# Moving mLSTM's half of the branch merge next to its gates, with the attention's halves made late

## The chip, the cores and the metric

The kernel runs on one core of a Trainium2 chip. The metric is the device time of one execution, in microseconds. Before the change the median of three runs is 1825.51 us (1820.42 to 1829.21).

## The reference

One block of a diffusion transformer over 512 tokens of width 1024 (with 256 context tokens): a token mixer with two branches, mLSTM (4 heads of 128) and window attention (8 query heads of 64, blocks of 128 tokens), a merge of the two behind sigmoid gates, a projection, and then PEER, a mixture of 16,384 tiny experts. The six modulation vectors (shift, scale and gate of both halves) come from `silu(c) @ w_ada`.

```python
mod = jax.nn.silu(cond) @ w + b                      # w: 1024 x 6144
pl = _split_in(h_lat @ w_in)
m_lat, m_ctx = _mlstm_branch(pl[:5], pc[:5], b_mgates, mlstm_norm_g, with_ctx_out)
a_lat, a_ctx = _attn_branch(pl[5:8], pc[5:8], q_g, k_g, sink, cos, sin, with_ctx_out)

def merge(m, a, gates):
    g_m, g_a = jnp.split(gates, 2, axis=-1)
    return (jax.nn.sigmoid(g_m) * (m @ w_bm) + jax.nn.sigmoid(g_a) * (a @ w_ba)) @ w_out

x = x + g1 * y_lat
x = x + g2 * _peer(_modulate(x, norm_ffn_g[layer], sh2, sc2), ...)
```

## The kernel before

**Arithmetic.** Every large product is float32 made of three passes: each operand is split into a high half (a copy rounded by ScalarE, `split`, L51) and a low half (the difference, L52, on VectorE or GpSimd), and `mm3` (L182 to L185) issues high x high, low x high and high x low. A tile product of 128 x 128 by 128 x 512 is therefore three matmuls.

**Stages.** (1) Norm, modulation and the projections of q, k, v and the attention's inputs. (2) The mLSTM heads (L503 to L537): for each head and direction a masked decay matrix `dm` (L510 to L513), two products per chunk and a running state; then the normaliser `den` and the norm over `num` (L541 to L559). (3) Attention (L586 to L643): the keys and queries are transposed and split; for each of four blocks `n` there are scores for 8 heads (L607, L608), a softmax (L615 to L626), transposes of the probabilities (L632) that are copied to `pTs` by VectorE and ScalarE in turn (L635, L637), and the product with the values (L640) into `po`; `split(ahi, alo, po)` ends a block. (4) Gates: `gate_proj` (L651) loads 0.5 MB of `w_gate`, splits it on ScalarE and GpSimd, and makes 24 matmuls into one PSUM bank: 4 output gates of mLSTM into `sigo`, then 16 branch gates (8 column tiles `n`, two branches `br` each), which are stored to DRAM (`sgd`, L681). After `sigo`, `num` is transposed (L670), scaled into `mt` (L672) and split to `mhi`, `mlo`. (5) Merge (L690 to L713): for each `n` the two gates are loaded again (`sgm`, L693), 0.5 MB of `w_br` is loaded and split, both branches' products are made (12 matmuls each), multiplied by the gates on VectorE (L710, L711), added on GpSimd (L712) and split to `zhi`, `zlo`. (6) Projection by `w_out` (L738 to L750): 24 matmuls for each of 8 column tiles, the residual (L749), squares, and a transposed copy. (7) The PEER stage follows and has its own written order.

**What sets the order.** Up to the PEER stage a scheduler orders each engine's instructions from the program order (earlier code has precedence) and from when it expects operands; at run time each engine and the DMA queue of SyncE (SP) work their list strictly in order. So gate products, written after the attention, fill TensorE's list between the attention's steps. Three background jobs are spread through these stages. `adas` (L138) loads one 0.5 MB row block of the modulation weights (`wada`, two buffers) and reduces it against `silp` on VectorE (`dot`, L134): 12 in the head loop (L540) and 20 in the attention loop (L643). `ahead(n)` (L352) prepares n tiles of the expert weights for PEER: load 0.5 MB (`sraw`, L358), high half on ScalarE (L360), low half on VectorE (L361), and, at the next call, store of the low half (`lows`, L355): 4 with the output gates, 16 with the branch gates, 8 in the merge, 8 in the projection. Weight tiles share one pool: `wraw` for loads, three buffers each of `whi` and `wlo`.

Of the kernel before, what the change touches and what calls it, by code (L numbers as in the profile page):

```python
# [38 lines left out]
def body(ctx, tc, A, out):  # L39
# [61 lines left out]
    silp = ga([128, 2, D], F32, "sil")  # L101

# [30 lines left out]
    def dot(w, i, col, keep=False):  # L133
        junk = wb([128, D], mybir.dt.bfloat16, "junk") if keep else w  # L134
        V.tensor_tensor_reduce(out=junk, in0=w, in1=silp[:, i], scale=1.0, scalar=0.0,  # L135
                               op0=ALU.mult, op1=ALU.add, accum_out=col)
# [428 lines left out]
    amask = ga([128, 640], F32, "amask")  # L565
# [25 lines left out]
    ahi, alo = ga([128, NB, 4, 128], F32R, "ahi"), ga([128, NB, 4, 128], F32R, "alo")  # L591
    for n in range(4):
# [49 lines left out]
        split(ahi[:, n], alo[:, n], po)  # L642
# [22 lines left out]
    g_m = load_const("g_mlstm", [128, 4])  # L665
    mhi, mlo = ga([128, NH, T], F32R, "mhi"), ga([128, NH, T], F32R, "mlo")
    for h in range(4):
        p = pst([128, T], "a1")
        for b in range(4):
            PE.transpose(p[:, b * 128:b * 128 + 128], num[0][:, b, h, 0:128], ident)  # L670
        mt = wb([128, T], F32, "mt")
        V.scalar_tensor_tensor(out=mt, in0=p, scalar=g_m[:, h:h + 1], in1=sigo[:, h], op0=ALU.mult, op1=ALU.mult)  # L672
        split(mhi[:, h], mlo[:, h], mt)


    sgd = dr.tile([8, 128, 2, T], F32, name="sgd")
    for n in range(8):
        for br in range(2):
            st = gen.tile([128, T], F32, name="sgs", tag="SGS", bufs=2)
            gate_proj(cG + br * 1024 + n * 128, st)  # L680
            nc.sync.dma_start(sgd[n, :, br], st)  # L681
            ahead(1)

# [6 lines left out]
    for n in range(8):  # L690
        sgs = [wb([128, T], F32, "sgm") for _ in range(2)]
        for br in range(2):
            nc.sync.dma_start(sgs[br], sgd[n, :, br])  # L693
        wbr = wp.tile([128, 2, 4, 128], F32, name="wraw", tag="wraw", bufs=WR)
        nc.sync.dma_start(wbr, A["w_br"][n])
        whi = wp.tile([128, 2, 4, 128], F32R, name="whi", tag="whi", bufs=3)
        wlo = wp.tile([128, 2, 4, 128], F32R, name="wlo", tag="wlo", bufs=3)
        split(whi, wlo, wbr)
        pz = []
        for br, (ah, al) in enumerate(((mhi, mlo), (ahi, alo))):  # L700
            p = pst([128, T])
            for k in range(4):
                if br == 0:
                    mh, ml = ah[:, k], al[:, k]
                else:
                    mh, ml = ah[:, :, k], al[:, :, k]
                mm3(p, whi[:, br, k], wlo[:, br, k], mh, ml, k == 0, k == 3)
            pz.append(p)
# [714 lines left out]
```

## Time and profile before

| | us |
|---|---|
| median of 3 runs | 1825.51 |
| profiled execution | 1829.64 |
| its span | 1827.7 |
| mLSTM heads (first `dm` to last) | 188.85 to 246.89 |
| attention block 1, first copy of probabilities | 341.33 |
| attention's last product ends | 446.4 |
| first merge matmul | 452.06 |
| last matmul of the `w_out` products starts | 554.00 |

The profiled execution is 4.1 us above the median, and 1.9 us of it lie around the span. All times in the trace are counted from the start of the span. "PE" is TensorE's matmuls, "PEld" its weight loads, "DVE" VectorE, "ACT" ScalarE, "POOL" GpSimd, "SP" SyncE, which issues most transfers. A row of the timeline gives the start, the duration and, in brackets, the idle time of the engine before it with what ended it. Matmuls are pipelined, so the distance between two starts, not the shown duration, is what one costs.

### The profile page before, as it was taken

The numbers are of one execution on the slowest core, as the hardware profiler recorded it, in microseconds if no ns is written. First come the engines' busy times: TensorE is split into PE (matmuls) and PEld (weight loads), VectorE is DVE, ScalarE is ACT, GpSimd is POOL, SyncE is SP. The second block draws the span as 40 slices with busy tenths as digits, with TensorE's granted clock in tenths as the row PEclk, the third lists the DMA queues.
The fourth block names the chain that finished last, engine by engine and source line by source line (L and its number), as shares of the span: only waits on it lengthen the run. The fifth ranks groups of instructions, "written<-read, shape, count | busy, mean of one in ns | idle before, by whom it ended". The sixth has DMA issues, their size and how long they took to land.

```text
span 1827.7 us, 25008 instructions
## 1 busy us (share of the span) xinstructions
PE 1738.9 (95%) x9079; PEld 1478.4 (81%) x9079; DVE 1420.8 (78%) x2756; ACT 765.2 (42%) x1139; POOL 481.9 (26%) x385
## 2 busy tenths in 40 slices
PE   8988888998998999989899999999999999999998
PEld 4877876663776898988889999999999999988886
DVE  6977977454655999988738888888888888896665
ACT  5442566463445335544433333333333333334332
POOL 0001123110203552000025454544454444520000
PEclk9999999996999999999899999999999999999999
DMA  9456645443695226799999999999999999987652
GB/s 370 134 202 211 203 164 190 161 150 115 239 304 185 81 93 213 237 344 323 305 352 361 353 340 343 353 339 349 349 327 369 337 341 354 339 344 266 229 211 101
DMA packets 181500, 483.51 MB, mean 265 GB/s; under 512 B 15616, under 2 KB 70400, under 8 KB 180480
## 3 DMA queue, kind: packets, MB, share of 16 engines
q1 hardware_dynamic: 93248, 312.82, 47.7%
q0 software_dynamic: 37008, 135.28, 20.2%
q10 hardware_dynamic: 51120, 33.82, 5.9%
q8 instruction: 71, 1.16, 0.2%
q14 instruction: 53, 0.43, 0.1%
HBM read 419.73 MB, written 62.13 MB: 264 GB/s over the span
## 4 chain that ended last, share of the span: by engine, by line
PE 70%; DMA 10%; DVE 10%; ACT 5%; issue 3%; POOL 1%; ACTq 1%; SPq 0%; DVEq 0%; POOLq 0%
PE pa L184 9%; PE pa L185 9%; PE pa L183 9%; PE pu L183 9%; PE pu L185 9%; PE pu L184 9%; DMA Gd<-stg 4%; PE ps L185 3%; PE ps L183 2%; PE ps L184 2%; PE a L640 2%; DMA wada<-in_w_adaT 2%; ACT stg L1024 1%; PE a L632 1%; DVE wada L135 1%
## 5 line engine op out<-in xcount | busy, mean ns | idle before, releaser
L183 PE MATMUL pu<-h2hi,whi 128*128 128x384 f32 (+1 forms) x1152 | 402.0, 349 | 9.5 <-ACT St L1128 8.1
L185 PE MATMUL pu<-h2lo,whi 128*128 128x384 f32 (+1 forms) x1152 | 395.6, 343 | 0.7 <-DVE h2lo L180 0.7
L184 PE MATMUL pu<-h2hi,wlo 128*128 128x384 f32 (+1 forms) x1152 | 394.7, 343 | 0.0
L795 DVE TENSOR_TENSOR wlo<-wraw,whi 128x1024 fp32r<-128x1024 f32 x210 | 256.8, 1223 | 106.0 <-ACT whi L784 104.4
L183 PE MATMUL pa<-whi,wh 128*128 128x512 f32 x768 | 299.6, 390 | 3.6 <-ACT wh L1140 3.6
L184 PE MATMUL pa<-whi,wl 128*128 128x512 f32 x768 | 301.4, 393 | 1.5 <-DVE wl L1144 1.4
L185 PE MATMUL pa<-wlo,wh 128*128 128x512 f32 x768 | 301.1, 392 | 0.0
L784 ACT ACTIVATE whi<-wraw 128x1024 fp32r<-128x1024 f32 x272 | 286.5, 1053 | 28.3 <-PE pa L184 12.9
L1071 POOL DMA_INDIRECT gath<-in_u,idx x128 | 163.7, 1279 | 414.6 <-DMA Sd<-St 237.8
L183 PEld LDWEIGHTS pu<-h2hi,whi 128*128 128x128 f32 x1152 | 218.0, 189 | 19.3 <-ACT St L1128 9.6
L184 PEld LDWEIGHTS pu<-h2hi,wlo 128*128 128x128 f32 x1152 | 217.9, 189 | 7.7
L185 PEld LDWEIGHTS pu<-h2lo,whi 128*128 128x128 f32 x1152 | 217.3, 189 | 7.4 <-DVE h2lo L180 2.6
L1071 POOL DMA_INDIRECT gath<-in_v,idx x128 | 162.4, 1269 | 180.3 <-DVE tokh L1103 165.6
L183 PEld LDWEIGHTS pa<-whi,wh 128*128 128x128 f32 x768 | 144.6, 188 | 33.0 <-ACT wh L1140 4.7
L184 PEld LDWEIGHTS pa<-whi,wl 128*128 128x128 f32 x768 | 144.5, 188 | 30.9 <-DVE wl L1144 2.5
L185 PEld LDWEIGHTS pa<-wlo,wh 128*128 128x128 f32 x768 | 144.6, 188 | 30.3
L1103 DVE SCALAR_TENSOR_TENSOR tokh<-gath,gw,tokh 128x1024 f32<-128x1024 f32 x127 | 162.7, 1281 | 0.6
L1095 DVE CUSTOM_DVE_ANT_0 gath<-gath,tokh 128x1024 f32<-128x1024 f32 x128 | 155.0, 1221 | 5.7 <-DMA gath<-in_u,idx 5.7
L1140 ACT ACTIVATE wh<-act 128x384 fp32r<-128x384 f32 x84 | 44.2, 526 | 256.8 <-DVE act L1136 256.8
L1128 ACT ACTIVATE act<-pu 128x384 f32<-128x384 f32 x84 | 41.2, 491 | 191.1 <-PE pu L185 191.1
L52 POOL TENSOR_TENSOR wlo<-wraw,whi 128x1024 fp32r<-128x1024 f32 x20 | 48.3, 2414 | 235.6 <-ACT whi L51 114.1
L51 ACT ACTIVATE whi<-wraw 128x1024 fp32r<-128x1024 f32 (+1 forms) x60 | 61.6, 1028 | 80.1 <-PE ps L184 28.5
(352 smaller groups left out, 2828.6 us busy)
## 6 DMA issues: line engine op xcount, KB each, us to landing
wraw<-in_uT SPq DMA_DIRECT2D x128, 512.0 KB, 6.4
wraw<-in_v SPq DMA_DIRECT2D x128, 512.0 KB, 6.4
Gd<-stg ACTq DMA_DIRECT2D x24, 1024.0 KB, 11.6
Gt<-Gd SPq DMA_DIRECT2D x32, 768.0 KB, 5.9
sraw<-in_uT SPq DMA_DIRECT2D x36, 512.0 KB, 4.2
lows<-sraw SPq DMA_DIRECT2D x36, 512.0 KB, 3.1
wlo<-lows SPq DMA_DIRECT2D x36, 512.0 KB, 5.5
wada<-in_w_adaT SPq DMA_DIRECT2D x32, 512.0 KB, 4.2
```

Of the source, the lines that this page charges most:

```text
L51: S.activation(hi, src, AF.Copy)
L52: (eng or V).tensor_tensor(out=lo, in0=src, in1=hi.bitcast(F32), op=ALU.subtract)
L183: PE.matmul(p, sh, mh, start=first, stop=False)
L184: PE.matmul(p, sl, mh, start=False, stop=False)
L185: PE.matmul(p, sh, ml, start=False, stop=last)
L784: S.activation(his[j], raws[j], AF.Copy)
L795: (G if pool else V).tensor_tensor(out=los[j], in0=raws.pop(j), in1=his[j].bitcast(F32), op=ALU.subtract)
L1071: G.indirect_dma_start(out=t, out_offset=None, in_=sparse["src"][s // 128], in_offset=bass.IndirectOffsetOnAxis(ap=sparse["idx"][:, s // 1 ...
L1095: V.tensor_tensor_reduce(out=t, in0=t, in1=tokh[:, 0], scale=1.0, scalar=0.0, op0=ALU.mult, op1=ALU.add, accum_out=gw[:, 0, s:s + 1])
L1103: V.scalar_tensor_tensor(out=tokh[:, 1], in0=t, scalar=gw[:, 0, s - 128:s - 127], in1=tokh[:, 1], op0=ALU.mult, op1=ALU.add)
L1128: S.activation(acts[i], p, AF.Gelu_apprx_tanh)
L1140: S.activation(wh, acts[i], AF.Copy)
```

## The change

Eight edits, all ahead of the PEER stage. (a) The 8 attention gates (`br` = 1) come first, each with `ahead(2)`; after four of them the transposes of `num` and the `mt` products. (b) Then, for each pair `q` of column tiles, two mLSTM gates, kept in SBUF, half a tile of weights, the mLSTM product, its multiplication by the gate, and a store of the product to `sgd` in place of the gate; `ahead(1)` each. (c) The merge makes the attention's product alone and adds the stored product. (d) That add is VectorE's, where GpSimd did it. (e) The projection loop has no `ahead`; the number of prepared tiles stays at 36 (4, 16, 8, 8). (f) Attention blocks 0 to 2 are copied to `ao` by ScalarE and split into `ahi`, `alo` only after the gates; block 3 is split from PSUM then. (g) The vector `silp[:, 0]` is copied into the tile of the attention mask, and the later `dot`s read the copy. (h) `w_br` is packed by branch and pair, 0.5 MB a load as before.

```diff
@@ -99,6 +99,7 @@
 
     warm = cst.tile([128, 1], F32, name="warm")
     silp = ga([128, 2, D], F32, "sil")
+    sils = [silp[:, 0], silp[:, 1]]
 
     def silu(i, nm):
         nc.sync.dma_start(silp[:, i], A[nm].to_broadcast([128, D]))
@@ -132,7 +133,7 @@
 
     def dot(w, i, col, keep=False):
         junk = wb([128, D], mybir.dt.bfloat16, "junk") if keep else w
-        V.tensor_tensor_reduce(out=junk, in0=w, in1=silp[:, i], scale=1.0, scalar=0.0,
+        V.tensor_tensor_reduce(out=junk, in0=w, in1=sils[i], scale=1.0, scalar=0.0,
                                op0=ALU.mult, op1=ALU.add, accum_out=col)
 
     def adas(a, b):
@@ -562,7 +563,10 @@
     banks(("m2", "m1"), a1=(2, 1), a2=(2, 2))
     aqt = ga([128, NB, 512], F32, "aqt")
     nc.sync.dma_start(aqt, aqd)
-    amask = ga([128, 640], F32, "amask")
+    amask_ = ga([128, 640 + D], F32, "amask")
+    amask = amask_[:, 0:640]
+    S.activation(amask_[:, 640:], silp[:, 0], AF.Copy)
+    sils[0] = amask_[:, 640:]
     nc.sync.dma_start(amask, A["amask"])
     sink = load_const("sink", [128, 8])
 
@@ -588,7 +592,12 @@
         for o in (a, z):
             V.tensor_tensor(out=kst[g][o, 1], in0=pk[a], in1=kst[g][a, 0].bitcast(F32), op=ALU.subtract)
 
-    ahi, alo = ga([128, NB, 4, 128], F32R, "ahi"), ga([128, NB, 4, 128], F32R, "alo")
+    ao = ga([128, 3, 4, 128], F32, "ao")
+    halves = {}
+
+    def attended(n, src):
+        split(halves["ahi"][:, n], halves["alo"][:, n], src)
+
     for n in range(4):
 
         lat = [b for b in (n - 1, n, n + 1) if 0 <= b < 4]
@@ -639,7 +648,8 @@
             for g in range(2):
                 PE.matmul(po[64 * g:64 * g + 64], akv[:, blk, 128 + 64 * g:192 + 64 * g], pts[g],
                           start=(i == 0), stop=(i == nk - 1))
-        split(ahi[:, n], alo[:, n], po)
+        if n < 3:
+            S.activation(ao[:, n], po, AF.Copy)
         adas(28 + 5 * n, 33 + 5 * n)
 
     def gate_tile(name):
@@ -663,23 +673,51 @@
         gate_proj(cO + h * 128, sigo[:, h])
         ahead(1)
     g_m = load_const("g_mlstm", [128, 4])
+
+    sgd = dr.tile([8, 128, 2, T], F32, name="sgd")
+
+    def branch_gate(n, br):
+        st = gen.tile([128, T], F32, name="sgs", tag="SGS", bufs=2)
+        gate_proj(cG + br * 1024 + n * 128, st)
+        return st
+
+    def branch_weights(br, q):
+        wbr = wp.tile([128, 2, 4, 128], F32, name="wraw", tag="wraw", bufs=WR)
+        nc.sync.dma_start(wbr, A["w_br"][br, q])
+        whi = wp.tile([128, 2, 4, 128], F32R, name="whi", tag="whi", bufs=3)
+        wlo = wp.tile([128, 2, 4, 128], F32R, name="wlo", tag="wlo", bufs=3)
+        split(whi, wlo, wbr)
+        return whi, wlo
+
+    def attention_gates(a, b):
+        for n in range(a, b):
+            nc.sync.dma_start(sgd[n, :, 1], branch_gate(n, 1))
+            ahead(2)
+
+    attention_gates(0, 4)
     mhi, mlo = ga([128, NH, T], F32R, "mhi"), ga([128, NH, T], F32R, "mlo")
     for h in range(4):
-        p = pst([128, T], "a1")
+        p = pst([128, T])
         for b in range(4):
             PE.transpose(p[:, b * 128:b * 128 + 128], num[0][:, b, h, 0:128], ident)
-        mt = wb([128, T], F32, "mt")
+        mt = gen.tile([128, T], F32, name="mt", tag="SGS", bufs=2)
         V.scalar_tensor_tensor(out=mt, in0=p, scalar=g_m[:, h:h + 1], in1=sigo[:, h], op0=ALU.mult, op1=ALU.mult)
         split(mhi[:, h], mlo[:, h], mt)
-
-
-    sgd = dr.tile([8, 128, 2, T], F32, name="sgd")
-    for n in range(8):
-        for br in range(2):
-            st = gen.tile([128, T], F32, name="sgs", tag="SGS", bufs=2)
-            gate_proj(cG + br * 1024 + n * 128, st)
-            nc.sync.dma_start(sgd[n, :, br], st)
+    attention_gates(4, 8)
+    for q in range(4):
+        sts = [branch_gate(2 * q + i, 0) for i in range(2)]
+        whi, wlo = branch_weights(0, q)
+        for i in range(2):
+            p = pst([128, T])
+            for k in range(4):
+                mm3(p, whi[:, i, k], wlo[:, i, k], mhi[:, k], mlo[:, k], k == 0, k == 3)
+            V.tensor_tensor(out=sts[i], in0=p, in1=sts[i], op=ALU.mult)
+            nc.sync.dma_start(sgd[2 * q + i, :, 0], sts[i])
             ahead(1)
+    for nm in ("ahi", "alo"):
+        halves[nm] = ga([128, NB, 4, 128], F32R, nm)
+    for n in range(4):
+        attended(n, ao[:, n] if n < 3 else po)
 
     V.tensor_tensor(out=mod[:, 16:48], in0=mod[:, 16:48], in1=b_ada[:, 16:48], op=ALU.add)
 
@@ -687,31 +725,21 @@
     banks(("a2", "a1", "ps"), ps=(6, 1), ps2=(1, 2))
     zh = [ga([128, 4, T], F32R, "zhi%d" % i) for i in range(2)]
     zl = [ga([128, 4, T], F32R, "zlo%d" % i) for i in range(2)]
-    for n in range(8):
-        sgs = [wb([128, T], F32, "sgm") for _ in range(2)]
-        for br in range(2):
-            nc.sync.dma_start(sgs[br], sgd[n, :, br])
-        wbr = wp.tile([128, 2, 4, 128], F32, name="wraw", tag="wraw", bufs=WR)
-        nc.sync.dma_start(wbr, A["w_br"][n])
-        whi = wp.tile([128, 2, 4, 128], F32R, name="whi", tag="whi", bufs=3)
-        wlo = wp.tile([128, 2, 4, 128], F32R, name="wlo", tag="wlo", bufs=3)
-        split(whi, wlo, wbr)
-        pz = []
-        for br, (ah, al) in enumerate(((mhi, mlo), (ahi, alo))):
+    for q in range(4):
+        whi, wlo = branch_weights(1, q)
+        for i in range(2):
+            n = 2 * q + i
+            sgs = [wb([128, T], F32, "sgm") for _ in range(2)]
+            for br in range(2):
+                nc.sync.dma_start(sgs[br], sgd[n, :, br])
             p = pst([128, T])
             for k in range(4):
-                if br == 0:
-                    mh, ml = ah[:, k], al[:, k]
-                else:
-                    mh, ml = ah[:, :, k], al[:, :, k]
-                mm3(p, whi[:, br, k], wlo[:, br, k], mh, ml, k == 0, k == 3)
-            pz.append(p)
-        z0 = wb([128, T], F32, "sgm")
-        V.tensor_tensor(out=sgs[0], in0=pz[0], in1=sgs[0], op=ALU.mult)
-        V.tensor_tensor(out=sgs[1], in0=pz[1], in1=sgs[1], op=ALU.mult)
-        G.tensor_tensor(out=z0, in0=sgs[0], in1=sgs[1], op=ALU.add)
-        split(zh[n // 4][:, n % 4], zl[n // 4][:, n % 4], z0)
-        ahead(1)
+                mm3(p, whi[:, i, k], wlo[:, i, k], halves["ahi"][:, :, k], halves["alo"][:, :, k], k == 0, k == 3)
+            z0 = wb([128, T], F32, "sgm")
+            V.tensor_tensor(out=sgs[1], in0=p, in1=sgs[1], op=ALU.mult)
+            V.tensor_tensor(out=z0, in0=sgs[0], in1=sgs[1], op=ALU.add)
+            split(zh[n // 4][:, n % 4], zl[n // 4][:, n % 4], z0)
+            ahead(1)
     g1 = mod[:, 16:24]
     x1T = Pair(F32, T, "x1T")
     x1d = dr.tile([128, 4, D], F32, name="x1d")
@@ -750,7 +778,6 @@
         square(x1T, n, acc, T)
         if n:
             residual_out(n - 1)
-        ahead(1)
     ahead(0)
 
 
@@ -1393,7 +1420,8 @@
     f["sink"] = np.tile(a["attn_sink"][0], (128, 1))
     cut = lambda m: m.reshape(-1, 128, m.shape[1] // 128, 128).transpose(2, 1, 0, 3)
     f["w_gate"] = ct(cut(np.concatenate([f["w_in"][:, 2048:2560], f["w_in"][:, 2832:]], axis=1)))
-    f["w_br"] = ct(np.stack([cut(a["w_branch_m"][0]), cut(a["w_branch_a"][0][hp])], 2))
+    pair = lambda m: cut(m).reshape(4, 2, 128, 4, 128).transpose(0, 2, 1, 3, 4)
+    f["w_br"] = ct(np.stack([pair(a["w_branch_m"][0]), pair(a["w_branch_a"][0][hp])]))
     f["w_out"] = ct(cut(a["w_out"][0]))
     f["w_in"] = ct(f["w_in"][:, 0:2832])
     f["w_q"] = ct(a["peer_w_query"][0].reshape(8, 128, 16, 128).transpose(2, 1, 0, 3).reshape(16, 128, 1024))
```

VectorE's list around the start of the mLSTM heads, before. `vL`, `kvc` and `ktok` are the copies of values and keys that the heads read, L135 is a `dot` on a `wada` tile, L510 the first instruction of head 0.

```order
L135 ISA wada_2460,mod<-wada_2460,sil 128x1024
L135 ISA mod 128x1
L486 COPY vL<-ps 128x4x128 x2
L135 ISA wada_2631,mod<-wada_2631,sil 128x1024
L135 ISA mod 128x1
L486 COPY kvc<-ps 128x4x128
L493 COPY ktok<-ps 128x512 x4
L135 ISA wada_2634,mod<-wada_2634,sil 128x1024
L135 ISA mod 128x1
L135 ISA wada_2637,mod<-wada_2637,sil 128x1024
L135 ISA mod 128x1
L510 TENSOR_TENSOR dm<-m_1478,pcr 128x512
```

The same place in the change (its line numbers are higher by one here):

```order
L467 TENSOR_TENSOR enm<-enm,gk 128x4x4 x2
L530 TENSOR_SCALAR kw<-kvc,wgt 128x128 x2
L362 TENSOR_TENSOR sraw<-sraw,shi 128x1024
L487 COPY vL<-ps 128x4x128 x2
L487 COPY kvc<-ps 128x4x128
L494 COPY ktok<-ps 128x512 x4
L362 TENSOR_TENSOR sraw<-sraw,shi 128x1024
L511 TENSOR_TENSOR dm<-m_1478,pcr 128x512
```

Of the 20 `dot`s of the attention loop, 13 stood ahead of this `dm` and 7 in the heads; now none does, because they read a tile that exists only after the heads. Seven stand between the last `dm` and block 0's softmax, and 13 from there to the first copy of block 1's probabilities. VectorE's list in the change where block 0's softmax ends and its probabilities are copied (L635 is the scaling, L644 the copy of probabilities, L136 a `dot`):

```order
L635 TENSOR_SCALAR sm<-sm,mx 128x512 x8
L136 ISA wada_2458,mod<-wada_2458,amask 128x1024
L136 ISA mod 128x1
L136 ISA wada_2628,mod<-wada_2628,amask 128x1024
L136 ISA mod 128x1
L644 COPY pTs<-a_2206 128x512
L362 TENSOR_TENSOR sraw<-sraw,shi 128x1024
L644 COPY pTs<-a_2215 128x512
L136 ISA wada_2631,mod<-wada_2631,amask 128x1024
L136 ISA mod 128x1
L362 TENSOR_TENSOR sraw<-sraw,shi 128x1024
```

Before, only `ahead`'s L361 stood between these copies.

TensorE's list at the end of the attention, before (L632 transposes probabilities of block 3, L640 multiplies them by the values, L670 transposes `num`):

```order
L632 MATMUL a_2764<-c_ident,sm 128x128 x4
L632 MATMUL a_2771<-c_ident,sm 128x128 x4
L640 MATMUL a_2646<-pTs,akv 64x512 x2
L632 MATMUL a_2780<-c_ident,sm 128x128 x4
L632 MATMUL a_2787<-c_ident,sm 128x128 x4
L640 MATMUL a_2646<-pTs,akv 64x512 x2
L670 MATMUL a_2969<-c_ident,num_1471 128x128 x4
```

and the same place in the change (L641 and L649 are those two; L184 to L186 on `mhi` are mLSTM's branch product, on `hhi` a gate):

```order
L649 MATMUL a_2643<-pTs,akv 64x512
L641 MATMUL a_2761<-c_ident,sm 128x128 x4
L185 MATMUL ps<-mhi,wlo 128x512
L186 MATMUL ps<-mlo,whi 128x512
L184 MATMUL ps<-mhi,whi 128x512
L185 MATMUL ps<-mhi,wlo 128x512
L641 MATMUL a_2768<-c_ident,sm 128x128 x4
L649 MATMUL a_2643<-pTs,akv 64x512
L186 MATMUL ps<-mlo,whi 128x512
L184 MATMUL ps<-hhi_211,whi 128x512
```

Counted in TensorE's list, from the first transposes of block 3 to its last value product there were 0 gate or branch matmuls before and there are 39 now. After that product come, before, 16 transposes and 384 matmuls (192 of the merge, 192 of the projection); now 132 of gates, 72 of mLSTM's branch product, 96 of the attention's and 192 of the projection, 492 in all.

SP's list in the change from the last store of a branch product on (L715 stores it, L734 loads gates and products for the merge, L359 and L356 are `ahead`'s load and store, L686 branch weights):

```order
L715 DMA sgd<-sgs 128x512
L356 DMA lows<-sraw 128x1024
L359 DMA sraw<-in_uT 128x1024
L734 DMA sgm<-sgd 128x512 x2
L359 DMA sraw<-in_uT 128x1024
L686 DMA wraw<-in_w_br 128x1024
L356 DMA lows<-sraw 128x1024
L734 DMA sgm<-sgd 128x512 x2
L356 DMA lows<-sraw 128x1024
L359 DMA sraw<-in_uT 128x1024
L734 DMA sgm<-sgd 128x512 x2
L359 DMA sraw<-in_uT 128x1024
```

All loads of the merge but the first branch weights stand behind that store, which waits for the last mLSTM product.

## Rows read from the trace of the kernel before

**Rows 1.** The profile page: engines' busy time, and the granted clock in 40 slices

```profile
PE 1738.9 (95%) x9079; PEld 1478.4 (81%) x9079; DVE 1420.8 (78%) x2756; ACT 765.2 (42%) x1139; POOL 481.9 (26%) x385
PEclk9999999996999999999899999999999999999999
```

**Rows 2.** Stretches: length, busy time (instructions) by engine, clock, DMA share, GB/s

```profile
189.00:247.00 58.00, 53.62 (x356) 47.28 (x355) 51.41 (x133) 34.56 (x74) 9.47 (x4) 0.99 0.56 188
247.00:341.00 94.00, 85.64 (x403) 62.40 (x401) 66.78 (x118) 62.24 (x100) 29.08 (x10) 0.96 0.45 157
341.00:418.00 77.00, 75.97 (x334) 47.88 (x332) 36.66 (x84) 42.62 (x71) 14.29 (x6) 1.00 0.47 167
418.00:446.00 28.00, 23.04 (x48) 7.74 (x47) 9.80 (x15) 6.87 (x9) 0.00 (x0) 0.52 0.39 141
453.00:507.00 54.00, 50.78 (x210) 40.11 (x209) 31.89 (x37) 19.51 (x24) 13.81 (x8) 0.97 0.66 228
507.00:555.00 48.00, 44.67 (x199) 34.90 (x199) 26.66 (x29) 22.82 (x30) 0.44 (x1) 1.00 0.90 302
```

**Rows 3.** VectorE's timeline ahead of the mLSTM heads

```profile
177.60 1.92 DVE L135 CUSTOM_DVE_ANT_0 wada<-wada,sil 128x1024 f32<-128x1024 f32 x1 [1.56 <-DMA wada<-in_w_adaT]
...
179.44 1.28 DVE L486 COPY vL<-ps 128x512 f32<-128x512 f32 x2
...
186.68 1.23 DVE L135 CUSTOM_DVE_ANT_0 wada<-wada,sil 128x1024 f32<-128x1024 f32 x1 [0.68 <-DMA wada<-in_w_adaT]
...
188.85 0.69 DVE L510 TENSOR_TENSOR dm<-m,pcr 128x512 f32<-128x512 f32 x1 [0.94 <-issue]
```

**Rows 4.** TensorE's waits from 174 to 190 us: for what, total, times, longest

```profile
PE m L504 <- DVE ktok L493: 3.0, 1, 3.0
```

**Rows 5.** VectorE's timeline: last `dm` of the heads, first `pTs` of blocks 0 and 1

```profile
246.89 0.69 DVE L513 TENSOR_TENSOR dm<-m,dm 128x512 f32<-128x512 f32 x1 [0.48 <-ACT dm L512]
...
308.49 0.69 DVE L635 COPY pTs<-a 128x512 f32<-128x512 f32 x1 [0.90 <-PE a L640]
...
341.33 0.69 DVE L635 COPY pTs<-a 128x512 f32<-128x512 f32 x1 [0.58 <-PE a L632]
```

**Rows 6.** The `dot`s (L135), 100 to 300 us: ns min/median/max, and idle before them

```profile
L135 DVE CUSTOM_DVE_ANT_0 wada<-wada,sil x27: 1205/1222/2830, 102.6 to 218.2; 128x1024 f32<-128x1024 f32 x27
...
  DMA wada<-in_w_adaT: 19.3, 10
```

**Rows 7.** TensorE's timeline: value products of block 0, and of block 3 to the merge

```profile
307.38 1.07 PE L640 MATMUL a<-pTs,akv 128*64 128x512 f32 x2
...
324.33 1.83 PE L640 MATMUL a<-pTs,akv 128*64 128x512 f32 x4
...
420.48 1.97 PE L640 MATMUL a<-pTs,akv 128*64 128x512 f32 x2
...
443.67 2.72 PE L640 MATMUL a<-pTs,akv 128*64 128x512 f32 x4
446.32 0.78 PE L670 MATMUL a<-c_ident,num 128*128 128x128 f32 x4
...
452.06 0.47 PE L183 MATMUL ps<-mhi,whi 128*128 128x512 f32 x1 [1.96 <-DVE mt L672]
```

**Rows 8.** TensorE's timeline: the last two matmuls of the projection

```profile
553.77 0.39 PE L184 MATMUL ps<-zhi,wlo 128*128 128x512 f32 x1
554.00 0.39 PE L185 MATMUL ps<-zlo,whi 128*128 128x512 f32 x1
```

**Rows 9.** A stretch of the projection, columns as in Rows 2

```profile
520.00:540.00 20.00, 19.36 (x88) 15.63 (x87) 9.48 (x11) 8.24 (x11) 0.00 (x0) 1.00 0.95 313
```

**Rows 10.** VectorE and GpSimd by line, 446 to 556 us: busy, mean ns, idle before

```profile
L361 DVE TENSOR_TENSOR sraw<-sraw,shi 128x1024 fp32r<-128x1024 f32 x14 | 17.1, 1223 | 12.9 <-ACT shi L360 12.9
...
L710 DVE TENSOR_TENSOR sgm<-ps,sgm 128x512 f32<-128x512 f32 x8 | 5.5, 686 | 4.8 <-PE ps L185 3.1 <-DMA sgm<-sgd 1.7
...
L712 POOL TENSOR_TENSOR sgm<-sgm 128x512 f32<-128x512 f32 x8 | 13.8, 1727 | 101.2 <-ACT shi L360 69.3 <-DVE sgm L711 31.9
```

## The prediction

> **What bounds the kernel now.** I read the page first: TensorE is busy for 95% of the span, at full clock but for one slice in the first quarter [rows 1]. The PEER stage, from some 565 us on, is such a stretch and the change leaves it alone, so only the time up to the last projection matmul (554.0 us, [rows 8]) can move. Next the stretches [rows 2], to see where TensorE loses time. From 341 to 418 us it is busy for 76 of 77 us: attention blocks 1 to 3, with gate products between, are bound by TensorE. From 418 to 446, block 3's transposes and value products have no gate left to run between: 28 us at a granted clock of 0.52, and a pair of value products takes 1.97 us there against 1.07 in block 0 [rows 7]. From 446 to 452 TensorE follows the chain through `mt` [rows 7]. The merge takes 54 us for 192 matmuls, the projection 48. Two matmuls start 0.23 us apart [rows 8], so 192 are 44 us: some 14 us are lost in both together, the projection with the transfers at a share of 0.90 [rows 2]. Last the waits and VectorE's timeline ahead of the heads: TensorE waits 3.0 us for `ktok` [rows 4], which stands behind `dot`s in VectorE's list, one of which waits for its `wada` load and holds the copies of `vL` [rows 3].
>
> **Part 1, heads.** The change's list has no `dot` ahead of the first `dm`. Four go from that stretch of the timeline: 3.4 us (wait, reduction, accumulator read: 176.0 to 179.4), twice 1.2, and 1.9 with its wait [rows 3], 7.8 us, and one `ahead` subtraction of 1.2 [rows 10] comes in: 6.5 us earlier, bounds 4 (TensorE's own work ahead of the heads) and 7.5. In the heads VectorE is busy for 51.4 of 58 us and TensorE for 53.6 [rows 2]; 7 `dot`s of 1.3 us with their accumulator read [rows 6] leave VectorE, 9 us. TensorE has little slack there, so I take 7. The last `dm`, at 246.9 [rows 5], comes 13.5 us earlier, at 233.4.
>
> **Part 2, the same `dot`s in attention.** All 20 now stand between the last `dm` and the first `pTs` of block 1. Before, that took 94.4 us [rows 5], VectorE busy for 66.8, TensorE for 85.6 [rows 2]. TensorE loses work here: from block 0's scores to block 1's value products there are 52 gate matmuls in its list against 164, 112 x 0.23 = 26 us less. VectorE gets 20 x 1.3 = 26 us more: 92.8. It becomes the engine that sets the pace, in order, so that a `dot` whose load is late holds the `pTs` copies behind it. `wada` has two buffers, and 10 of 27 `dot`s waited, 19.3 us in all [rows 6]; for 20 that would be 14 us. Some of these waits fall where VectorE waits anyway (it idles for 27 of the 94 us now). Bounds: 3 and 19 us (the second with TensorE slow as well); I take 11, nearer to the observed share. 104 us, so the first `pTs` of block 1 is at 337.4 instead of 341.3: of 13.5 us, 4 are left.
>
> **Part 3, blocks 1 to 3.** From there to the last value product it took 105 us [rows 5, 7]. The gates and branch matmuls between are as many as before (180 in either list), but 39 now lie in block 3's last part. What TensorE did from 418 to 446 is 23.0 us at half clock, 12 at full; with 76 ahead of it that is 88, and I add 7 for waits on the copies: 95, 10 less. Bounds: 91 (3 us of waits) and 103 (block 3 still at half clock for most of it). VectorE, busy for 46 us of these 105, has 8 more subtractions at most and stays clear. Attention ends at 432.4 instead of 446.4. The `num` chain of 5.7 us (446.3 to 452.1, [rows 7]) disappears under gates. The three copies to `ao` replace the high halves that ScalarE made, and the late splits run beside gates: nothing.
>
> **Part 4, after attention.** 492 matmuls are left instead of 384. Only 24 of the 96 of mLSTM's product lie inside the attention; 72 and 132 gate matmuls come after it: 204 x 0.23 = 47, with restarts 48 us, to 480.4. Then the attention's 96, 22 us if their inputs are there. They are not all: the merge's loads stand behind the last product store in SP's list, which waits for the last mLSTM matmul. From that row to the last pair of gate loads 12.5 MB must move: 6 loads and 6 stores of `ahead`, 16 gate or product tiles of 0.25 MB, 2 branch and 3 projection weights. At 313 GB/s for a share of 0.95 [rows 9] full use is 330 GB/s, 38 us; then multiply, add and split, 3 us. So the last `zhi` comes 41 us after 480.4, at 521.4, and the projection has 171 matmuls left by then (its first tile runs but for the last three): 39.3 us. Bounds: 25 us instead of 41 (TensorE alone, 22 + 3) and 45. The Trainium skill, "DMA: Bandwidth & Descriptors", section "Where 436 GB/s comes from", has some 358 GB/s of HBM for a core as the binding limit. The rows show less, 330; by the page the 38 us would be 35 and the end 3 us sooner.
>
> GpSimd's adds (1.73 us each) become 0.69 on VectorE [rows 10], 1 us each in a chain that transfers cover: nothing, with 1 us of gain as the bound. The projection loses its 8 `ahead`s, so its weights meet a freer queue; that is why I count it at 0.23 a matmul with no loss, where it lost 4 us.
>
> **Sum.** 233.4 + 104 + 95 + 48 + 41 + 39.3 = 560.7, against 554.0: 6.7 us later. In profiled terms 1829.6 becomes 1836.3; the profiled execution stands 4.1 us above the median, so against the median of 1825.5 I forecast 1832.2. A change under 0.5%, 9.1 us, can hardly be told from none here, so this is nominally "same".
>
> **Rivals.** (A) *The tail and the heads pay in full.* The `dot`s slip into waits of VectorE, so blocks 0 and 1 take no longer than before: attention ends at 233.4 + 94.4 + 95 = 423, and transfers keep up: 48 + 25 + 39 more, 535, 19 us sooner. With half of the second, 543, 11 us sooner: 1814.5. For it: TensorE has 26 us less to do in blocks 0 and 1, and the DMA share there is 0.45. Against it: VectorE's sum of 92.8 alone is as long as the 94 us, and 12.5 MB behind one store. Point of decision: the `pTs` of block 1 ahead of 330 us.
>
> (B) *Slower: blocks 0 and 1 starve TensorE.* What block 3 shows, products at half clock between waits for `pTs` [rows 2, 7], moves to blocks 0 and 1, which have lost their fillers. Block 0's value part has the same 8 products as block 3's, which took 28 us; now it lasts some 18 (308.5 to 326, [rows 5, 7]). 10 us more, and all four `dot`s between its copies late: attention ends at 443 and the rest follows, 571 or 17 us later: 1842.5. It decides if the granted clock of block 0's value part is 0.5. The Trainium skill, "TensorE: Matmul & The Clock Gate", section "HAM oscillation — how this bites in real kernels", says that short bursts of matmuls between waits leave the array at the lower clock time after time; that speaks for this rival and against the change, and 418 to 446 agrees with it at 0.52.
>
> (C) *Nothing moves*: the loads bound merge and projection before (0.90) and bound them still, and whatever the attention gains is waited for there. That gives 554 to 558, 1825 to 1829; it shares its band with the forecast, since the bytes after the attention hardly shrink.
>
> **How the numbers follow.** Forecast 0.36, (C) 0.10, (A) 0.22, (B) 0.32. The forecast's own band is +/- 8 us about 1832, so a quarter of it is past the upper limit of 1834.6. (A) is mostly under 1816.4. Faster 0.22, same 0.38, slower 0.40. The range takes (A)'s half payment and (B) with late loads (45 us instead of 41 and 5 more in the attention, 1851): 1811 to 1852.
>
> **What would show it.** Right: first `dm` near 182, last near 233; no wait of `vL` behind a `dot`; 20 `dot`s between there and block 1's copies with waits on `wada` of some 10 us, and the first `pTs` of block 1 at 335 to 340; block 3's end at full clock, with 39 matmuls between; no wait of TensorE for `mt`; some 48 us of gates and mLSTM products, then gaps of TensorE on loads of `sgm` and weights in the merge; the last `zhi` 35 to 45 us after the last mLSTM matmul; the last projection matmul near 561. Wrong: attention ending ahead of 425 or after 445, or a merge without gaps.

## The result and the profile after

The changed kernel takes 1845.16 us (1841.42 to 1845.98, three runs) against 1825.51: a ratio of 1.0103, 95% interval 1.0063 to 1.0143. It is slower. In a second series of five rounds it was 1842.31 against 1826.01, ratio 1.0080 (1.0051 to 1.0110). The two profiled executions stand 11.8 us apart (1841.42 and 1829.64).

The stretches of the changed kernel, cut where its stages change (columns as in [rows 2]):

```profile
179.00:233.00 54.00, 52.65 (x359) 46.78 (x358) 40.61 (x120) 33.79 (x75) 7.07 (x3) 1.00 0.31 114
233.00:334.00 101.00, 73.51 (x295) 47.58 (x293) 88.85 (x154) 50.03 (x86) 19.67 (x6) 0.78 0.59 198
334.00:411.00 77.00, 73.81 (x303) 44.59 (x304) 44.08 (x91) 41.97 (x72) 12.44 (x5) 0.93 0.51 178
411.00:434.00 23.00, 23.00 (x95) 12.77 (x94) 10.98 (x19) 10.05 (x13) 5.59 (x2) 1.00 0.60 206
434.00:484.00 50.00, 49.22 (x215) 40.00 (x214) 19.36 (x19) 19.64 (x23) 9.53 (x4) 1.00 0.66 239
484.00:525.00 41.00, 31.26 (x112) 23.24 (x111) 28.23 (x34) 17.11 (x21) 0.00 (x0) 0.83 0.94 327
525.00:567.00 42.00, 41.97 (x196) 33.99 (x194) 19.90 (x20) 14.72 (x22) 4.81 (x2) 1.00 0.57 185
```

Against [rows 2]: the last part of the attention, 28 us at a clock of 0.52 before, is 23 us at 1.00. But the stretch from the heads to block 1's copies, 94 us with 85.6 us of matmuls at 0.96, is 101 us with 73.5 at 0.78. And after the attention there is a stretch of 41 us (484 to 525) in which TensorE is busy for 31 at 0.83 while the DMA engines are at 0.94.

VectorE's timeline of the changed kernel, the rows that answer to [rows 3] and [rows 5]:

```profile
179.39 0.69 DVE L511 TENSOR_TENSOR dm<-m,pcr 128x512 f32<-128x512 f32 x1 [1.07 <-PE m L509]
...
231.61 0.69 DVE L514 TENSOR_TENSOR dm<-m,dm 128x512 f32<-128x512 f32 x1 [0.59 <-ACT dm L513]
...
290.89 0.69 DVE L644 COPY pTs<-a 128x512 f32<-128x512 f32 x1
...
333.49 0.69 DVE L644 COPY pTs<-a 128x512 f32<-128x512 f32 x1
```

and TensorE's, answering to [rows 7] and [rows 8]: a pair of value products of block 3, the last matmul of mLSTM's product, the first and the last of the projection:

```profile
420.26 1.07 PE L649 MATMUL a<-pTs,akv 128*64 128x512 f32 x2
...
480.01 0.39 PE L186 MATMUL ps<-mlo,whi 128*128 128x512 f32 x1
...
515.17 0.54 PE L184 MATMUL ps<-zhi,whi 128*128 128x512 f32 x1 [2.60 <-ACT whi L51]
...
566.14 0.39 PE L186 MATMUL ps<-zlo,whi 128*128 128x512 f32 x1
```

The last projection matmul comes at some 566 instead of 554 us. From there to the end it is 1273.5 us in the trace of the changed kernel and 1273.7 in the one before, so all of the 12 us lies ahead of PEER, as assumed. Single executions scatter by several microseconds (before: 1815 to 1834 in 29 runs), so a time below is compared in two ways: by the ratio, and in the trace by distances from the first `dm` of the heads, since that `dm` itself moves by up to 5 us between executions whose lists are the same up to there. The rows of the table are differences of times rounded to 0.1 us.

| us, from the traces | before | changed | dots early | mt behind 8 gates | both | all four, z in place |
|---|---|---|---|---|---|---|
| run | | | e_nog | e_mt8 | e_mt8_nog | e_all_z |
| first `dm` at | 188.8 | 179.4 | 189.0 | 179.2 | 188.0 | 187.2 |
| first to last `dm` | 58.1 | 52.2 | 57.0 | 52.2 | 58.0 | 57.8 |
| to first `pTs` of block 1 | 94.4 | 101.9 | 97.6 | 100.4 | 96.5 | 96.3 |
| to the end of attention | 105.1 | 99.9 | 98.9 | 101.1 | 97.8 | 99.3 |
| to the last mLSTM matmul | (50.8) | 46.6 | 44.4 | 44.8 | 29.0 | 29.0 |
| to the last `zhi` | 9.2 | 44.8 | 43.8 | 44.5 | 45.0 | 27.2 |
| to the last projection matmul | 47.6 | 41.3 | 40.7 | 39.9 | 39.7 | 42.9 |
| first `dm` to that matmul | 365.2 | 386.7 | 382.4 | 382.9 | 366.0 | 352.5 |

(In the kernel before, mLSTM's matmuls are part of the merge, so the two rows from the end of attention to the last `zhi` are one: 60.0 us.)

### The profile page after: what moved, and what is told of

Same layout as the page of the kernel before. It is cut to its first block, busy times and chain, and to the rows that moved or that the text cites. A ratio compares the mean times of both kernels' runs of the same rounds, so it can differ in the third digit from the quotient of the medians.

```text
span 1839.7 us, 24999 instructions
## 1 busy us (share of the span) xinstructions
PE 1746.1 (95%) x9079; PEld 1485.2 (81%) x9079; DVE 1429.0 (78%) x2764; ACT 760.4 (41%) x1138; POOL 468.9 (25%) x377
## 4 chain that ended last, share of the span: by engine, by line
PE 69%; DMA 8%; DVE 7%; ACT 3%; issue 2%; POOL 0%; SPq 0%; ACTq 0%; DVEq 0%; POOLq 0%
PE pa L185 9%; PE pa L186 9%; PE pa L184 9%; PE pu L184 9%; PE pu L186 8%; PE pu L185 8%; DMA Gd<-stg 6%; PE ps L184 3%; PE ps L185 3%; PE ps L186 3%; PE a L649 2%; ACT stg L1051 1%; PE a L641 1%; DMA sraw<-in_uT 1%; PE pg L907 1%
## 5 line engine op out<-in xcount | busy, mean ns | idle before, releaser
L184 PE MATMUL pu<-h2hi,whi 128*128 128x384 f32 (+1 forms) x1152 | 404.5, 351 | 11.7 <-ACT St L1155 10.3
L186 PE MATMUL pu<-h2lo,whi 128*128 128x384 f32 (+1 forms) x1152 | 397.7, 345 | 0.2 <-DVE h2lo L181 0.2
L811 ACT ACTIVATE whi<-wraw 128x1024 fp32r<-128x1024 f32 x272 | 286.7, 1054 | 39.1 <-PE pa L185 12.2
L186 PE MATMUL pa<-wlo,wh 128*128 128x512 f32 x768 | 300.4, 391 | 0.0
L184 PE MATMUL pa<-whi,wh 128*128 128x512 f32 x768 | 299.0, 389 | 0.2
L184 PEld LDWEIGHTS pu<-h2hi,whi 128*128 128x128 f32 x1152 | 219.6, 191 | 21.8 <-ACT St L1155 11.7
L186 PEld LDWEIGHTS pu<-h2lo,whi 128*128 128x128 f32 x1152 | 219.1, 190 | 6.2 <-DVE h2lo L181 0.9
L186 PEld LDWEIGHTS pa<-wlo,wh 128*128 128x128 f32 x768 | 144.1, 188 | 29.9
L184 PEld LDWEIGHTS pa<-whi,wh 128*128 128x128 f32 x768 | 144.2, 188 | 29.5 <-ACT wh L1167 1.3
L1167 ACT ACTIVATE wh<-act 128x384 fp32r<-128x384 f32 x84 | 44.2, 526 | 254.4 <-DVE act L1163 240.4
L52 POOL TENSOR_TENSOR wlo<-wraw,whi 128x1024 fp32r<-128x1024 f32 x20 | 51.9, 2599 | 299.7 <-ACT whi L51 299.7
L1155 ACT ACTIVATE act<-pu 128x384 f32<-128x384 f32 x84 | 41.3, 492 | 189.0 <-PE pu L186 188.9
L822 POOL TENSOR_TENSOR wlo<-wraw,whi 128x1024 fp32r<-128x1024 f32 x26 | 62.4, 2398 | 173.1 <-ACT whi L811 173.1
```

The lines of the kernel that those rows point to most:

```text
L52: (eng or V).tensor_tensor(out=lo, in0=src, in1=hi.bitcast(F32), op=ALU.subtract)
L184: PE.matmul(p, sh, mh, start=first, stop=False)
L186: PE.matmul(p, sh, ml, start=False, stop=last)
L811: S.activation(his[j], raws[j], AF.Copy)
L822: (G if pool else V).tensor_tensor(out=los[j], in0=raws.pop(j), in1=his[j].bitcast(F32), op=ALU.subtract)
L1155: S.activation(acts[i], p, AF.Gelu_apprx_tanh)
```

## The experiments

**The changed kernel again (r_after).** No edit.

> The changed kernel once more, in five rounds beside the kernel before. In the profiled executions it ends its projection 12 us later and everything behind it takes the same time, while the medians differ by 19.7 us. My theory, that all of the difference lies ahead of PEER, expects 10 to 14 us (ratio 1.0055 to 1.0077); a rival, that something in PEER also got slower, expects 18 us or more (1.010).

Ratio 1.0080 (1.0051 to 1.0110), 14.6 us. In its trace the last projection matmul comes 386.3 us after the first `dm` (386.7 in the first trace) and 1272.8 us before the end. PEER is not slower in either trace. The ratio falls between the two expectations, nearer to the first, and its interval holds the 12 us of the traces. The size of the loss is 12 us by the traces and 15 to 19 by the two ratios.

**`ahead` out of the merge (e_aout).** Theory 1 was the prediction's: the bytes behind the last product store hold the merge. The 8 calls of `ahead` go from the merge's loop back to the projection's.

```diff
             split(zh[n // 4][:, n % 4], zl[n // 4][:, n % 4], z0)
-            ahead(1)
...
             residual_out(n - 1)
+        ahead(1)
```

> Only the 8 calls of ahead in the merge are moved back into the projection loop. Theory 1 (the merge is held by the bytes behind the last product store: 12.5 MB, 41 to 45 us): some 8 MB leave that stretch, the last zhi comes about 25 to 30 us after the last mLSTM matmul instead of 45, the projection carries the bytes at a DMA share near 0.95 and loses up to 4 us; 11 to 15 us faster than the changed kernel, level with the kernel before. Theory 2 (the loss is that blocks 0 and 1 are starved: TensorE busy 74 of 101 us at a clock of 0.79): nothing there changes, under 3 us.

Ratio 1.0054 (1.0035 to 1.0074), by the ratios some 5 us faster than the changed kernel beside it, and 379.4 us from the first `dm`, 7 less than 386.7. The attention's products were done 23 us after the last mLSTM matmul (32 in the changed kernel), but the last `zhi` came only 39.6 us after it (44.8). The direction is theory 1's, the size half of it. Two stretches of its merge:

```profile
484.00:508.00 24.00, 23.22 (x101) 18.60 (x100) 14.76 (x18) 9.51 (x12) 0.00 (x0) 1.00 0.68 235
508.00:524.00 16.00, 10.08 (x41) 7.10 (x39) 9.79 (x13) 4.12 (x6) 0.00 (x0) 1.00 0.97 338
```

The DMA engines stand at 0.68 while the attention's products run, and at 0.97 after. So in the first part it is not the bytes alone that hold the loads.

**Dots early (e_nog).** The copy of `silp` is undone; the `dot`s return to their places ahead of the heads and in them.

```diff
-    amask_ = ga([128, 640 + D], F32, "amask")
-    amask = amask_[:, 0:640]
-    S.activation(amask_[:, 640:], silp[:, 0], AF.Copy)
-    sils[0] = amask_[:, 640:]
+    amask = ga([128, 640], F32, "amask")
```

> Only the copy of silp into the mask's tile is undone, so that the 20 dots stand ahead of the heads and in them as before the change. Theory 1: the heads end near 247 again, blocks 0 and 1 lose 26 us of VectorE work, the first pTs of block 1 comes at 327 to 333 instead of 333.5 and everything after follows: 0 to 6 us faster than the changed kernel. Theory 2: the dots in blocks 0 and 1 are the cost, with the clock back at 1.0 there; 10 us or more faster than the changed kernel.

Ratio 1.0087 (1.0055 to 1.0119): no gain. That is no more than the low end of theory 1, whose first `pTs` of block 1 at 327 to 333 us came at 343.6, and against theory 2. The first `dm` is late again and the heads last 57.0 us instead of 52.2; the stretch to block 1's copies takes 97.6 instead of 101.9. So what the late `dot`s cost in blocks 0 and 1 (4 us) they give back in the heads (5), and they start the heads some 8 us sooner: in the seven executions with late `dot`s the first `dm` came between 179.2 and 184.3 us, in the six with early ones between 187.2 and 192.4. But the clock in blocks 0 and 1 did not come back:

```profile
246.00:344.00 98.00, 77.80 (x314) 49.97 (x314) 69.33 (x126) 52.67 (x91) 21.15 (x7) 0.81 0.42 149
```

VectorE has 29 us to spare there again, and TensorE still does 77.8 us at 0.81 where it did 85.6 before [rows 2].

**Both (e_nog_aout).**

> Both undone: dots early and the last 8 calls of ahead in the projection. Theory 1: 11 to 15 us from the merge plus 0 to 6 us from the dots, 11 to 20 us faster than the changed kernel, so 0 to 8 us faster than the kernel before (ratio 0.996 to 1.000). Theory 2: no more than the dots alone give.

Ratio 1.0057 (1.0028 to 1.0085); 379.2 us from the first `dm`, as e_aout. By the ratios that is 4 us faster than the changed kernel, where theory 1 had 11 to 20, and e_aout alone gave 5. The two do not add.

**What starves blocks 0 and 1.** The trace of e_nog shows it. The transposes of `num`, `mt`, the split of `mt`, and the next gate matmul:

```profile
295.33 1.32 PE L699 MATMUL ps<-c_ident,num 128*128 128x128 f32 x8 [1.15 <-DVE mt L701]
...
336.47 0.50 PE L184 MATMUL ps<-hhi,whi 128*128 128x512 f32 x1 [1.22 <-DVE mt L701]
```

```profile
294.52 1.41 DVE L701 SCALAR_TENSOR_TENSOR mt<-ps,c_g_mlstm,sigo 128x512 f32<-128x512 f32 x2
...
328.64 0.62 ACT L51 ACTIVATE mhi<-mt 128x512 fp32r<-128x512 f32 x1
```

In the rows between, no gate matmul runs from 295 to 336 us. The change took `num`'s transposes from the attention's PSUM banks to the two banks of the gates, and `mt` to the two `SGS` buffers of the gates. Two heads' `mt` fill both buffers at 296, the next two heads' transposes both banks; the split that frees them stands behind block 0 in ScalarE's list, 33 us later. In the changed kernel there is a second hindrance. SP's waits there from 232 to 334 us (for what: total, times, longest), SP's list, and TensorE's gate matmuls:

```profile
SPq L142 <- DVE mod L136: 23.4, 9, 6.5
SPq L142 <- DVE mx L630: 18.1, 2, 14.0
```

```profile
267.40 0.33 SPq L694 DMA_DIRECT2D sgd<-sgs  x1
281.69 1.61 SPq L142 DMA_DIRECT2D wada<-in_w_adaT  x2
284.18 1.53 SPq L356 DMA_DIRECT2D lows<-sraw  x2
290.05 0.33 SPq L661 DMA_DIRECT2D wraw<-in_w_gate  x1
```

```profile
266.35 0.39 PE L186 MATMUL ps<-hlo,whi 128*128 128x512 f32 x1
...
294.85 0.79 PE L184 MATMUL ps<-hhi,whi 128*128 128x512 f32 x1 [0.19 <-ACT whi L51]
```

A `wada` load waits 14 us for VectorE, whose earlier `dot` has to free the buffer; the gate's weights stand behind it in SP's list, and TensorE has no gate for 28 us. From here on this is called theory 3: either hindrance alone keeps the gates out of blocks 0 and 1, the stretch does not get shorter for it (the attention's own chain sets its length), and each matmul left out is paid in full afterwards.

**mt behind all eight attention gates, dots early (e_mt8_nog).**

```diff
-    attention_gates(0, 4)
+    attention_gates(0, 8)
...
-    attention_gates(4, 8)
```

> The dots as before the change, and the num transposes with mt moved from behind four attention gates to behind all eight. Theory 3 (in blocks 0 and 1 the early mt chain holds both PSUM banks and both buffers of the gates, and late dots hold the gate loads in SP's list; so gates are missing there, TensorE runs at half clock, and 26 us of gate matmuls are paid after the attention): the gap in gates from 295 to 336 us goes, TensorE's clock there is back near 1.0, the attention from the first dm takes 253 to 258 us as in every run so far, but only 127 instead of 204 matmuls are left after it; the last projection matmul comes 369 to 374 us after the first dm (before the change 365, changed kernel 387, dots early 382): 8 to 13 us faster than with the dots early alone. Theory 1 (only the merge counts): the gates moved into blocks 0 and 1 lengthen them by what they save later, under 4 us.

Ratio 1.0025 (1.0005 to 1.0045), and 366.0 us from the first `dm`: 16.4 less than with the `dot`s early alone, more than expected; by the ratios 11 us faster than that run, as expected. The attention takes 252.3 us from the first `dm` in this run and 253.5 in e_nog, with 67 matmuls more inside it; what follows it up to the last mLSTM matmul falls from 44.4 to 29.0.

```profile
246.00:342.00 96.00, 83.32 (x377) 58.68 (x377) 69.76 (x120) 64.90 (x102) 23.92 (x8) 0.93 0.54 191
```

63 matmuls more than in e_nog's row above, the clock at 0.93, and 1 us less time (96.5 against 97.6). They were free there, and the 67 that no longer follow the attention account for the 15.4 us at 0.23 us each. Theory 3 holds.

**mt behind eight gates, dots late (e_mt8).** The same edit on the changed kernel.

> Only mt behind all eight attention gates; the dots stay late. With the run that moved the dots alone (no gain) and the run that moved both (16 us sooner from the first dm) this completes the square. Theory 3 as it stands (either holds the gates of blocks 0 and 1 by itself): only 8 more matmuls fit into the attention, the last projection matmul comes 383 to 387 us after the first dm against 387 in the changed kernel, and gate loads still wait in SP's list behind wada loads. Rival: mt alone is the hindrance, the dots are harmless: 368 to 374.

Ratio 1.0091 (1.0064 to 1.0119), 382.9 us from the first `dm`; the stretch to block 1's copies (232 to 332 us) has 291 matmuls, 295 in the changed kernel. SP again waits for a `wada` buffer, from 267.5 to 280.8, and TensorE has no gate from 266 to 293. Each hindrance alone is enough: 386.7 with both, 382.4 and 382.9 with one, 366.0 with none. That is why e_nog showed nothing.

**The merge's loads on GpSimd's list (e_gq).**

```diff
-                nc.sync.dma_start(sgs[br], sgd[n, :, br])
+                G.dma_start(sgs[br], sgd[n, :, br])
```

> Only the loads of gates and products in the merge go from SP's list to GpSimd's, which has nothing else to do there. If the order of SP's list holds them (each stands behind loads of ahead that wait for a free weight buffer): the last zhi comes 25 to 32 us after the last mLSTM matmul instead of 45, and the end 10 to 15 us sooner than in the changed kernel. If it is the bytes (12.5 MB at 330 GB/s, as I predicted): still 40 us or more, and under 4 us.

Ratio 1.0089 (1.0059 to 1.0118), the last `zhi` 44.2 us after the last mLSTM matmul. With SP's order out of the way the stretch reads:

```profile
485.00:529.00 44.00, 35.29 (x137) 26.32 (x136) 31.00 (x37) 19.21 (x22) 5.33 (x10) 0.92 0.94 348
```

15.3 MB at 348 GB/s and a share of 0.94. So SP's order is not what holds the merge when all 8 calls of `ahead` are in it. The share of 0.94 speaks for the bytes, as the prediction had it, but the run does not separate them from the buffers of the loads, for which GpSimd waits 38.8 us here; more room for the loads was tried only without the calls of `ahead` (e_all_z).

**The same, with `ahead` out of the merge (e_gq_aout).**

> Those loads on GpSimd's list, and the last 8 calls of ahead in the projection. Order theory: last zhi 25 to 28 us after the last mLSTM matmul (39.6 with the calls moved alone), the projection 41 to 46 us with their bytes; 14 to 18 us faster than the changed kernel. Byte theory: 33 to 40 us, no more than 4 us faster than with the calls of ahead moved alone.

Ratio 1.0027 (1.0007 to 1.0047), the last `zhi` 35.8 us after the last mLSTM matmul, inside the byte theory's 33 to 40 and not at the order theory's 25 to 28. But by the ratios the run is 5 us faster than e_aout, a little more than the byte theory allowed; 372.9 us from the first `dm`, 6.5 less than with `ahead` moved alone (3.8 of them to the last `zhi`; 2.6 lie in the attention, where nothing was edited, and are not explained). With fewer bytes SP's order costs some 4 us, and something else is left, since this merge has the DMA engines at 0.79.

**All four (e_all).** Dots early, `mt` behind eight gates, the merge's loads on GpSimd's list, `ahead` in the projection.

> All four: dots early, mt behind eight gates, the merge's loads on GpSimd's list, the last 8 calls of ahead in the projection. Theory 3 with the order theory: attention 255 us from the first dm, 29 us of gates and products, 25 to 28 to the last zhi, 41 to 46 of projection: the last matmul 350 to 358 us after the first dm, 7 to 15 us faster than the kernel before (ratio 0.992 to 0.996). If blocks 0 and 1 grow by what is moved into them, 362 or more: level with before.

Ratio 0.9956 (0.9935 to 0.9977), 355.8 us from the first `dm`: faster than either kernel, and theory 3's part came as expected. The order theory's did not: the last `zhi` is again 35.7 us after the last mLSTM matmul, not 25 to 28. The waits of GpSimd from 440 to 510 us show what is left:

```profile
POOL sgm L730 <- DVE sgm L736: 36.4, 5, 19.8
```

**The sum written over the gate (e_all_z).** This run has the four changes of e_all and one more. In e_all the loads waited for buffers: each column tile took three, two for the loads and one for their sum.

```diff
-            z0 = wb([128, T], F32, "sgm")
+            z0 = sgs[0]
```

> The four changes together, and the sum z0 written over the gate tile instead of into a third buffer. In the run of the four, each pair of loads waited for VectorE to free the buffers of three tiles before (GpSimd waited 36 us for it), and the last zhi came 35.8 us after the last mLSTM matmul, 12.5 after the last attention product. If the buffers hold it: 25 to 32 us, 4 to 10 us faster than the four (0.990 to 0.994 of the kernel before). If the bytes hold it: 34 to 36 us, no gain.

Ratio 0.9934 (0.9913 to 0.9956); the last `zhi` comes after 27.2 us, 4 after the last attention product. The buffers held it. Of these 8.5 us only 3 reach the last projection matmul (352.5 us from the first `dm` against 355.8): in e_all 42 projection matmuls had run before the last `zhi`, here 17, and the rest came after it. By the ratios the gain over e_all is 4 us, and the two intervals overlap. The merge and the projection, to be set against the 41 us at 0.83 and the 42 us of the changed kernel:

```profile
463.00:492.00 29.00, 28.22 (x123) 22.58 (x122) 21.84 (x29) 12.76 (x16) 3.77 (x7) 1.00 0.79 272
492.00:535.00 43.00, 43.00 (x201) 35.22 (x200) 28.05 (x31) 22.47 (x28) 1.30 (x1) 1.00 0.91 313
```

TensorE is busy throughout, and the projection carries the 8 MB of `ahead` at a share of 0.91. Its 43 us for 41 are 8 more matmuls after the last `zhi`, not the bytes. This version is 1814.71 against 1825.92 us: 12 us faster by the ratio than the kernel before, some 27 faster than the changed one, which was timed in another series.

**The add back on GpSimd (e_gadd).**

```diff
-            V.tensor_tensor(out=z0, in0=sgs[0], in1=sgs[1], op=ALU.add)
+            G.tensor_tensor(out=z0, in0=sgs[0], in1=sgs[1], op=ALU.add)
```

> Only the merge's add goes back to GpSimd. I costed this edit at nothing because transfers cover it: within 2 us of the changed kernel, the last zhi 44 to 47 us after the last mLSTM matmul. A rival (VectorE in order is what makes the last zhi late): 3 us or more either way.

Ratio 1.0103 (1.0078 to 1.0128), 387.1 us from the first `dm` (386.7), the last `zhi` after 46.3. These are within 1.5 us of the changed kernel's first trace, and the intervals of the ratios overlap, so the add's engine is worth nothing that these runs can tell.

## Why the prediction held, and where it was off

The forecast, 1832.2 us and 6.7 us of loss in the trace, has the right sign; the trace shows 12.0. The measured 1845.2 is in the range of 1811 to 1852, but outside the 8 us that the forecast gave itself, and nearer to rival (B)'s 1842.5. The range reaches that far only because (B) is in it, and (B)'s mechanism did not come, so that the number was caught is in part luck. Step by step:

- *Heads.* First `dm` at 179.4, from 188.85: 9.5 us sooner, where 6.5 with a bound of 7.5 was forecast; some of it is the scatter of that point (181.7 in the repeat). First to last `dm` 52.2 instead of 58.1, 6 for the forecast 7. Last `dm` at 231.6 (233.4 forecast).
- *Blocks 0 and 1.* 101.9 us for the forecast 104, VectorE busy for 88.9 of 101 (92.8 forecast), first `pTs` of block 1 at 333.5 (337.4). The sum came out, for the wrong reason. The forecast took 11 us for `dot`s that wait for a late `wada` load. In VectorE's waits from 232 to 334 us these are 2.5 us in three waits, so that the stretch is within 2 us of the forecast is luck. Taking the 26 us of `dot`s out again (e_nog) shortened the stretch by 4 us, not to what the remaining work needs: in all runs here it lasts 94 to 103 us, with 26 us of gates more or less in it and 26 us of `dot`s more or less. And the late `dot`s hurt less through the copies behind them on VectorE than through the gate loads behind their own loads in SP's list, a queue that I had not followed there.
- *Blocks 1 to 3.* 99.9 us for 95. Block 3's value products ran at full clock, 1.07 us a pair instead of 1.97, as forecast; the stretch ahead of it had TensorE at 0.93, not at full clock. Attention ended at 433.4 (432.4).
- *To the last mLSTM matmul.* 46.6 us for 48, at 480.0 for 480.4.
- *Merge.* 44.8 us to the last `zhi` for 41, so this term was 3.8 us too small. The rate was right (327 GB/s at 0.94, forecast 330 at full use); the bytes were not. In the 45 us from 480 to 525 the trace has 331 GB/s, 14.9 MB, not 12.5. The count itself was 0.5 MB too high: the first pair of gate loads was issued at 429.7 us, ahead of the last product store, where the section on the change has only branch weights. By their issue times, transfers issued shortly ahead of that store (481.2) were probably still on their way, and two `w_out` loads and four residual tiles followed from 518 to 523, close behind the last pair of gate loads (517.1). What each of these is worth was not separated.
- *Projection.* 41.3 us after the last `zhi` for 39.3. The matmuls left take 39.1 us (166 in the trace), and the 24 transposes of `x1T` between them 2.1 us, a term that the sum left out; no two starts are more than 0.5 us apart there. The `w_out` weights came late, so that the projection's first matmul ran only at 515.2 and the next ones at half clock, but that lies ahead of the last `zhi`.
- *All terms.* Merge and projection are 5.8 us over the forecast; the terms ahead of them come out 0.4 us below it, but by cancelling: 1.8, 2.1 and 1.4 us below, and 4.9 above in blocks 1 to 3.
- *The add, the copies to `ao`, the late splits.* Costed at nothing. e_gadd bears that out for the add; the copies and the late splits were not tried alone.

Rival (A), blocks 0 and 1 as fast as before, fell: the first `pTs` of block 1 came at 333.5, not ahead of 330. So did (C), with 566 us for 554 to 558. Rival (B) was right that the missing fillers would bring the clock down in blocks 0 and 1 (0.78), but not where it put this. It was to be decided by a clock of 0.5 in block 0's value part, which is the middle one of these rows; the low clock lies ahead of it and behind it:

```profile
267.00:295.00 28.00, 17.24 (x53) 10.41 (x53) 24.38 (x53) 13.53 (x25) 0.13 (x1) 0.61 0.45 149
288.00:310.00 22.00, 20.95 (x68) 9.61 (x67) 15.66 (x23) 2.96 (x5) 2.36 (x1) 0.79 0.70 246
318.00:334.00 16.00, 6.86 (x18) 2.80 (x18) 15.01 (x27) 8.44 (x16) 3.13 (x1) 0.59 0.58 197
```

Nor does this lengthen the stretch by (B)'s 10 us: with the `dot`s early it is 97.6 us at 0.81 and 96.5 at 0.93. By the rule of the Trainium skill that I set beside it ("TensorE: Matmul & The Clock Gate", section "HAM oscillation — how this bites in real kernels") the clock should fall there, and the rows agree. In these two traces it cost some 1 us; that the chain of copies and softmax sets the pace is the reading of these runs, not a run of its own.

What the prediction counted but did not name as the lever is the 108 matmuls that move behind the attention. I took them as given by the list. They are there because two gate buffers were lent to `mt` and because the late `dot`s' loads stand ahead of the gate loads; with both mended, 77 of them go back into a stretch that does not grow. From the first `dm` that is 20.7 us less than in the changed kernel, of which some 8 are lost again because the early `dot`s start the heads later; by the ratios (1.0080 and 1.0025) 10 us of the loss go. Shown by runs: the square of e_nog, e_mt8 and e_mt8_nog, and for the merge e_gq, e_all and e_all_z. Not tried: `mt` in buffers of its own beside the eight gates, late `dot`s whose loads stand behind the gate loads, and the mended attention with the merge of the kernel before.

## What to carry to other kernels

When work is moved so that it fills an engine in one place, ask what it now holds there: here a buffer pair and two PSUM banks lent to a short chain shut out the filler that had kept TensorE busy at no cost. Where filler runs beside a chain that sets its own pace, a matmul left out saves nothing there and costs its full price later, so count what is left behind the chain rather than what the chain lost. Two hindrances that each suffice hide one another: an experiment that removes one alone and shows nothing does not clear it.

## What was not expected of the hardware

In blocks 0 and 1, with the `dot`s early, the stretch took 97.6 us at a granted clock of 0.81 with 314 matmuls and 96.5 us at 0.93 with 377: a lower clock in a stretch is not by itself a loss. And the transfers of the merge reached 348 GB/s over 44 us when 4 MB of the loads came from GpSimd's list (327 GB/s over 41 us with all in SP's), without a gain that the ratios show (1.0089 and 1.0080).
